# S5 preparation of a two-block network: cut into pieces behind the weight splits, with 32 powers and GpSimd's queue for its loads

## The chip, the cores and the metric

One core of one Trainium2 chip runs the whole program. The metric is the device time of one execution in microseconds. The kernel's times below are three executions; one more was taken by the hardware profiler, and every row shown comes from that one.

## The reference

Input `x` is 256 tokens by 1024. The first block has two layers, each `FFN1 -> mixer -> FFN2` with norms around them; the second block is attention, a dense FFN, attention again and a mixture of eight experts. All weights are fp32, and almost all of the time is spent on products of those weights with 256 tokens.

```python
def first_block(x, ...):
    h = x
    for i in range(DEPTH):                       # DEPTH = 2
        f = swiglu(rmsnorm(h, ffn1_pre_g[i]), ffn1_w_gate[i], ffn1_w_up[i], ffn1_w_down[i])
        h = h + 0.5 * rmsnorm(f, ffn1_post_g[i])
        m = mixer(rmsnorm(h, mix_pre_g[i]), ...)
        h = h + rmsnorm(m, mix_post_g[i])
        f = swiglu(rmsnorm(h, ffn2_pre_g[i]), ffn2_w_gate[i], ffn2_w_up[i], ffn2_w_down[i])
        h = h + 0.5 * rmsnorm(f, ffn2_post_g[i])
    return h

def s5_branch(u, lam_re, lam_im, b_re, b_im, c_re, c_im, log_step, d_skip, w_glu):
    ...
    lam_bar = jnp.exp(lam * step)                # 64 groups x 64 states, complex
    b_bar = ((lam_bar - 1.0) / lam)[..., None] * lax.complex(b_re, b_im)
    bu = jnp.einsum("blgc,gnc->blgn", ug, b_bar)
    _, states = lax.associative_scan(combine, (a_elems, bu), axis=1)   # s[t] = lam_bar * s[t-1] + bu[t]
    y = jnp.real(jnp.einsum("blgn,gcn->blgc", states, c))
```

The S5 branch of the mixer depends on the layer's input only through `u`. Everything made from `lam`, `step`, `b` and `c` alone is the "S5 preparation" of this text: it can be computed before the mixer, and both kernels do it during FFN1 (and, for one part of layer 1, during layer 0's FFN2).

## The kernel before

**The stream of weights.** A weight comes from HBM in units of 512 KB (128 x 1024 fp32). SP's queue loads a unit into a buffer `raw` (L1571 `unit`), ScalarE (ACT) copies it to `hi` (L1576), VectorE (DVE) computes `lo = raw - hi` (L1577), and TensorE (PE) makes three products per tile: `hi*hi`, `lo*hi`, `hi*lo` (L1585 to L1587, and L1591 to L1593 where weights are the stationary side). A `raw` buffer is free for the next load when its `lo` is done. `hi` and `lo` go to tiles called `big`, `part`, `hi`, `lo`; the number behind a name is the tile.

**An FFN** (`swiglu`) runs gate and up product in six chunks of columns (c0 to c5, 44 units together), then the down product (`stream_k`, 22 units d0 to d21). Chunk c0 uses `lead_b`, the others `stream_b`. Each `stream_b` unit calls `self.beside()`, which takes one step of a generator `self.side` and constrains its instructions to stand behind the unit's split (`issue_after(self.last_lo)`). The down product's last six units (`tail`) are multiplied with the first 128 tokens as they arrive and with the other 128 afterwards.

**Order.** The program is written in the order of data; a scheduler then fixes each engine's instruction order, and the queue of each engine that issues transfers, under the `issue_after` constraints. Engines run their own orders strictly in sequence. A transfer that waits for a buffer holds up what stands behind it on the same queue.

**S5 preparation in FFN1 of layer l** is a generator (`prep`) with few, large steps, placed by a table `PREP`: after chunk or unit so-and-so, take the next step. Its steps:

- `mix_prep`, layer 0 only: constants, `exp`, `sin`, `cos`, small powers (many DVE operations of 128 x 64, names `cut`, `FL`, L103 to L274), ending in the write of `lsd` to DRAM (L279, GpSimd's queue).
- `s5_wb` for each quarter q of the groups: loads `s5B` and `s5L` (L331, L333, SP's queue), four `tensor_tensor` on GpSimd (POOL, L341 to L344), and a write `Wd` (L346, GpSimd's queue). There is one buffer `s5B` and one `s5L`, so the next quarter's load waits until the `Wd` write has landed.
- `s5_cb`: loads of `s5c` (SP) and `s5b` (GpSimd) for a quarter.
- `s5_ct`: six DVE operations into `s5CF` (L372 to L377), one buffer; two ACT copies into `s5bq` (L380).
- `s5_products`: 32 pairs of small PE products into `zfa` (L396), a copy to `s5u` (L401), DVE operations that make `T` (L404 to L414), and two writes `Td` (L419, L420, GpSimd's queue).
- `s5_powers_prep(l, h)` for each half h of the groups: powers 1 to 63 of a complex number by doubling in six levels, 36 DVE operations on tiles `E` and `Et` (L301 to L303), and three writes `Ed` (L305, GpSimd's queue).

Layer 1's powers are made in layer 0's FFN2 after units d2 and d8. After FFN1 `norms` follows: its first `tensor_tensor` with `pow` on POOL (L1748), `xn` (L1771), transposes (`trfa`, L1730), and then the mixer's first product. The functions that the change touches:

Of the kernel before, what the change touches and what calls it, by code (L numbers as in the profile page):

```python
# [51 lines left out]

PREP = (
    ("c0 c1 c2 c3 c4 d0 d3 d6 d9 d12".split(), "d0 d4 d10 d15".split()),
    ("c1 c2 c4 d1 d6".split(), "c4 d1 d6 d11".split()),
)
# [22 lines left out]
class Mixer:  # L79
# [201 lines left out]
    def s5_powers_prep(self, l, h):  # L281


        g = self.nc.gpsimd
# [1 line left out]
        Ed = self.Ed[l, h] = self.dram.tile([3, P, 1024], F32, tag="Ed", name=self.nm("Ed"), bufs=4)
        if True:
            E = [self.slot("B", "E").rearrange("p (a i) -> p a i", i=64) for _ in range(3)]
            Et = self.slot("B", "Et").rearrange("p (k a i) -> p k a i", k=2, i=32)
            x, y = Et[:, 0], Et[:, 1]  # L290
# [1 line left out]
            g.memset(E[2][:, :, 0], 0.0)
            self.nc.scalar.copy(E[2][:, :, 1:], self.s4len[:, ls].unsqueeze(2).to_broadcast([P, 16, 63]))
            for r in range(2):
                g.memset(E[r][:, :, 0], 1.0 - r)
                self.nc.scalar.copy(E[r][:, :, 1], self.s4dir[:, r, ls])
            for n in (1, 2, 4, 8, 16, 32):
                k = min(n, 63 - n)
                b = [e[:, :, n : n + 1].to_broadcast([P, 16, k]) for e in E[:2]]
                for r, op in ((0, ALU.subtract), (1, ALU.add)):  # L300
                    tt(x[:, :, :k], E[0][:, :, 1 : k + 1], b[r], op=ALU.mult)  # L301
                    tt(y[:, :, :k], E[1][:, :, 1 : k + 1], b[1 - r], op=ALU.mult)
                    tt(E[r][:, :, n + 1 : n + 1 + k], x[:, :, :k], y[:, :, :k], op=op)  # L303
# [1685 lines left out]
```

## Time and profile before

| what | value |
|---|---|
| three executions | 2934.03, 2936.93, 2939.28 us; median 2936.93 |
| the profiled execution's own time | 2936.55 us |
| span of its trace | 2934.5 us |
| mean granted TensorE clock | 0.981 |
| busy, share of span: PE / DVE / ACT / POOL | 96% / 74% / 57% / 7% |

FFN1 of layer 0 runs from 11.9 (its first matmul) to 240.7, gate and up until 150.4; the mixer's first matmul is at 247.7. The other FFNs of the first block, with the same number of units: layer 0's FFN2 from 663.8 (down product from 792.6, end 852.6) and layer 1's FFN1 from 855.3 (down product from 988.3, end 1056.5, mixer's first matmul 1059.8). A row of windows gives, for a stretch, the busy time of each engine and the number of its instructions; a wait is put down to what ended it last. PEclk is the granted clock of TensorE as a share of its full 2.4 GHz. Durations of neighbouring pipelined matmuls overlap.

### The profile page before, as it was taken

How to read it: one execution, taken by the hardware profiler on the slowest of the kernel's cores; microseconds unless marked ns; L12 is line 12 of the kernel's file. 1: busy time of each engine (PE TensorE's matmuls, PEld its weight loads, DVE VectorE, ACT ScalarE, POOL GpSimd, SP SyncE). 2: the span in 40 equal slices, each digit the busy share in tenths (PEclk: the TensorE clock that was granted, in tenths of full speed). 3: DMA queues.
4: the chain of work that ended last, by engine and by line, in shares of the span. 5: the costliest groups of instructions: out<-in, count | busy, mean ns of one | idle time of the engine just before them, and what ended most of it. 6: DMA issues, size and time to landing. Idle time of an engine off the chain costs nothing. (4 is left out here: it accounts for less than half of the span.)

```text
span 2934.5 us, 49144 instructions
## 1 busy us (share of the span) xinstructions
PE 2814.3 (96%) x19040; PEld 2508.2 (85%) x19040; DVE 2181.6 (74%) x3043; ACT 1674.2 (57%) x2389; POOL 206.0 (7%) x257
## 2 busy tenths in 40 slices
PE   8979999999999999999999999999999999999997
PEld 7968888999979888888999898987678888888886
DVE  5886877765667758777755566555589999999997
ACT  5434456545445444475554445445377777777776
POOL 2140001000004100010000000000000000000000
PEclk9999999999999999999999999999899999999998
DMA  7677565576567775656855646654589999999993
GB/s 238 199 250 242 160 204 164 197 227 188 184 223 249 241 221 174 194 155 196 264 171 180 215 154 192 186 192 132 184 279 356 343 361 361 343 359 356 354 344 145
DMA packets 350928, 687.88 MB, mean 234 GB/s; under 512 B 32672, under 2 KB 121952, under 8 KB 350688
## 3 DMA queue, kind: packets, MB, share of 16 engines
q1 hardware_dynamic: 336592, 637.42, 65.9%
q0 software_dynamic: 13952, 46.74, 4.8%
q8 instruction: 151, 2.47, 0.3%
q14 instruction: 89, 0.73, 0.1%
q10 hardware_dynamic: 144, 0.52, 0.0%
HBM read 658.05 MB, written 26.54 MB: 233 GB/s over the span
## 5 line engine op out<-in xcount | busy, mean ns | idle before, releaser
L1577 DVE TENSOR_TENSOR lo<-raw,hi 128x1024 fp32r<-128x1024 f32 x646 | 788.6, 1230 | 296.8 <-ACT hi L1576 285.1
L1576 ACT CAST hi<-raw 128x1024 fp32r<-128x1024 f32 x646 | 674.9, 1048 | 455.6 <-PE accmo L1587 84.6
L1586 PE MATMUL accmo<-lo,xg 128*128 128x512 f32 (+1 forms) x768 | 289.7, 378 | 2.3 <-DVE lo L1577 2.3
L1587 PE MATMUL accmo<-hi,xg 128*128 128x512 f32 (+1 forms) x768 | 285.2, 372 | 0.0
L1585 PE MATMUL accmo<-hi,xg 128*128 128x512 f32 (+1 forms) x768 | 274.0, 373 | 1.4 <-ACT hi L1576 1.4
L1577 DVE TENSOR_TENSOR big<-raw,big 128x1024 fp32r<-128x1024 f32 x147 | 184.9, 1259 | 110.2 <-ACT big L1576 109.3
L1576 ACT CAST big<-raw 128x1024 fp32r<-128x1024 f32 x147 | 153.7, 1049 | 168.0 <-issue 31.1
L1577 DVE TENSOR_TENSOR part<-raw,part 128x1024 fp32r<-128x1024 f32 x111 | 135.3, 1223 | 85.5 <-ACT part L1576 83.1
L1576 ACT CAST part<-raw 128x1024 fp32r<-128x1024 f32 x111 | 116.1, 1050 | 114.2 <-DMA raw<-in_ffn_w_gate_dram 17.4
L1586 PEld LDWEIGHTS accmo<-lo,xg 128*128 128x128 f32 x768 | 144.6, 188 | 32.3 <-DVE lo L1577 5.6
L1585 PEld LDWEIGHTS accmo<-hi,xg 128*128 128x128 f32 x768 | 144.6, 188 | 28.1 <-ACT hi L1576 2.6
L1587 PEld LDWEIGHTS accmo<-hi,xg 128*128 128x128 f32 x768 | 144.8, 189 | 22.5
L1586 PE MATMUL accmo<-lo,th 128*128 128x512 f32 x352 | 138.0, 392 | 0.0
L1587 PE MATMUL accmo<-hi,th 128*128 128x512 f32 x352 | 137.7, 391 | 0.0
L1577 DVE TENSOR_TENSOR lo<-big,hi 128x1024 fp32r<-128x1024 f32 x88 | 106.6, 1223 | 10.7 <-ACT hi L1576 7.6
L1585 PE MATMUL accmo<-hi,th 128*128 128x512 f32 x352 | 109.2, 391 | 0.0
L1576 ACT CAST hi<-big 128x1024 fp32r<-128x1024 f32 x88 | 92.7, 1054 | 27.0 <-PE accmo L1587 26.7
L1592 PE MATMUL accfa<-xh,lo 128*128 128x256 f32 x352 | 99.8, 284 | 0.0
L1591 PE MATMUL accfa<-xh,hi 128*128 128x256 f32 x352 | 99.7, 283 | 0.0
L1593 PE MATMUL accfa<-xl,hi 128*128 128x256 f32 x352 | 99.7, 284 | 0.0
L1577 DVE TENSOR_TENSOR lo<-more,hi 128x1024 fp32r<-128x1024 f32 x68 | 82.3, 1223 | 7.0 <-ACT hi L1576 5.0
L1576 ACT CAST hi<-more 128x1024 fp32r<-128x1024 f32 x68 | 71.4, 1053 | 19.3 <-PE accmo L1587 17.8
(993 smaller groups left out, 8603.3 us busy)
## 6 DMA issues: line engine op xcount, KB each, us to landing
raw<-in_w_gu_moe_dram SPq DMA_DIRECT2D x190, 512.0 KB, 5.3
raw<-in_w_in_dram SPq DMA_DIRECT2D x128, 512.0 KB, 4.4
raw<-in_w_down_moe_dram SPq DMA_DIRECT2D x94, 512.0 KB, 5.6
raw<-in_ffn_w_gate_dram SPq DMA_DIRECT2D x88, 512.0 KB, 4.1
raw<-in_ffn_w_up_dram SPq DMA_DIRECT2D x88, 512.0 KB, 4.3
raw<-in_ffn_w_down_dram SPq DMA_DIRECT2D x88, 512.0 KB, 4.2
big<-in_w_gu_moe_dram SPq DMA_DIRECT2D x60, 512.0 KB, 5.7
more<-in_w_gu_moe_dram SPq DMA_DIRECT2D x46, 512.0 KB, 5.7
```

The lines of the kernel that those rows point to most:

```text
L1576: nc.scalar.copy(hi, raw)
L1577: self.last_lo = nc.vector.tensor_tensor(lo, raw, hi.bitcast(F32), op=ALU.subtract).ins
L1585: mm(ps, lh, rh, start=first, stop=False)
L1586: mm(ps, lh, rl, start=False, stop=False)
L1587: self.last_mm = mm(ps, ll, rh, start=False, stop=last).ins
L1591: mm(ps, lh, rh, start=first, stop=False)
L1592: mm(ps, ll, rh, start=False, stop=False)
L1593: self.last_mm = mm(ps, lh, rl, start=False, stop=last).ins
```

## The change

The steps of S5 preparation get smaller and go to `beside()`, which now also runs in the down product:

- `PREP` and `product()` are gone. Layer 0's `prep` is cut into 47 steps, layer 1's into 20. After chunk c0 (layer 0) or c1 (layer 1), every unit's split may be followed by one step; the down product's last six units have no such place. Steps that are left over after FFN1 are drained behind the last split.
- `s5_powers_prep(l)` makes powers 1 to 31 for all 32 groups at once: five levels, 30 DVE operations. Two tables of 64 columns per half are then put together on ACT: columns 32 to 63 are the powers 0 to 31, columns 1 to 31 the conjugates in reverse (`E[r][:, hs, :0:-1]`). The table is thus centred about column 32, which leaves the recurrence's result as it was. In layer 0 it comes before the quarters; layer 1's is in layer 0's FFN2 from c4 on.
- Loads of `s5B`, `s5L` and `s5c` are issued on GpSimd's queue.
- `T = K * jm` moves from DVE to ACT. The products are a step of their own.

```diff
     def s5_prep(self, I, l):
@@
         cb = [self.s5_cb(I, l, 0)]
-        yield
+        if l == 0:
+            yield from self.s5_powers_prep(0)
         for q in range(4):
             self.s5_wb(I, l, q)
             if q < 3:
                 cb.append(self.s5_cb(I, l, q + 1))
-            self.late.append(self.s5_ct(l, q, *cb.pop(0)))
-            yield
-            if l == 0 and q in (1, 2):
-                self.s5_powers_prep(0, q - 1)
-                yield
+            yield from self.s5_ct(l, q, *cb.pop(0))
@@
-        nc.sync.dma_start(B, I["s5_bT"][l, q])
+        nc.gpsimd.dma_start(B, I["s5_bT"][l, q])
         ld = self.lsd[:, p0 : p0 + 8].rearrange("k a x -> k (a x)")
-        nc.sync.dma_start(Lb, ld.unsqueeze(1).to_broadcast([8, 16, 1024]))
+        nc.gpsimd.dma_start(Lb, ld.unsqueeze(1).to_broadcast([8, 16, 1024]))
@@
-        self.nc.sync.dma_start(cc, I["s5_cT"][l, q])
+        self.nc.gpsimd.dma_start(cc, I["s5_cT"][l, q])
@@
-        nc.vector.tensor_scalar_mul(T, K, self.jm[:, 0:1])
+        nc.scalar.activation(T, K, AF.Copy, scale=self.jm[:, 0:1])
@@
             if i < nk - kk * tail:
+                self.beside()
+            if i < nk - kk * tail:
                 go(0, u, k0)
                 go(1, u, k0)
-                if aside:
-                    aside(f"d{i}")
@@
-        steps = self.prep(I, l)
-        at = PREP[l]
-
         def aside(w):
             if w == f"c{l}":
                 self.ring_drop((6, 7), (8, 9))
-            if w in at[1]:
-                self.product()
-            if w in at[0]:
-                with self.tc.issue_after(self.last_lo), self.tc.issue_after(self.last_pow.ins):
-                    next(steps, None)
-
-        return self.swiglu(*xT, *w, aside)()
+                self.side = self.prep(I, l)
+                if l == 0:
+                    with self.tc.issue_after(self.last_lo), self.tc.issue_after(self.last_pow.ins):
+                        next(self.side)
+
+        banks = self.swiglu(*xT, *w, aside)()
+        with self.tc.issue_after(self.last_lo):
+            for _ in self.side:
+                pass
+        return banks
```

The powers, new:

```python
        for n in (1, 2, 4, 8, 16):
            k = min(n, 31 - n)
            b = [e[:, :, n : n + 1].to_broadcast([P, 32, k]) for e in E]
            for r, op in ((0, ALU.subtract), (1, ALU.add)):
                tt(x[:, :, :k], E[0][:, :, 1 : k + 1], b[r], op=ALU.mult)
                ...
        for h in range(2):
            ...
            for r in range(2):
                g.memset(F[r][:, :, 0], 0.0)
                cp(F[r][:, :, 32:], E[r][:, hs])
                self.nc.scalar.activation(F[r][:, :, 1:32], E[r][:, hs, :0:-1], AF.Copy, scale=1.0 - 2.0 * r)
            g.memset(F[2][:, :, 0], 0.0)
            cp(F[2][:, :, 1:], self.s4len[:, ls].unsqueeze(2).to_broadcast([P, 16, 63]))
            for r in range(3):
                g.dma_start(Ed[r], F[r].rearrange("p a i -> p (a i)"))
```

The scheduler's order changes in three places more than the diff tells. First, DVE at the start of the program, where `xn_126` and `xn_153` are the first norm's outputs for the two halves of the tokens, and `raw_177` to `raw_223` are the first five units. Before:

```order
L1747 SCALAR_TENSOR_TENSOR sm_122<-sm_116,sm_119 128x1
L1771 SCALAR_TENSOR_TENSOR xn_126<-h_99,sm_123,gn_114 128x512 x2
L1747 SCALAR_TENSOR_TENSOR sm_149<-sm_143,sm_146 128x1
L1771 SCALAR_TENSOR_TENSOR xn_153<-h_100,sm_150,gn_114 128x512 x2
L1577 TENSOR_TENSOR big_170<-raw_177,big_170 128x1024
L1720 TENSOR_TENSOR xl_113<-tr_128,xh_112 128x4x128
L1720 TENSOR_TENSOR xl_113<-tr_136,xh_112 128x4x128
L1577 TENSOR_TENSOR big_170<-raw_187,big_170 128x1024
L1577 TENSOR_TENSOR lo_199<-raw_197,hi_198 128x1024
```

Now:

```order
L1770 SCALAR_TENSOR_TENSOR sm_122<-sm_116,sm_119 128x1
L1600 TENSOR_TENSOR big_170<-raw_177,big_170 128x1024
L1600 TENSOR_TENSOR big_170<-raw_187,big_170 128x1024
L1600 TENSOR_TENSOR lo_199<-raw_197,hi_198 128x1024
L1600 TENSOR_TENSOR lo_211<-raw_209,hi_210 128x1024
L1600 TENSOR_TENSOR lo_225<-raw_223,hi_224 128x1024
L1794 SCALAR_TENSOR_TENSOR xn_126<-h_99,sm_123,gn_114 128x512 x2
L1770 SCALAR_TENSOR_TENSOR sm_149<-sm_143,sm_146 128x1
L1794 SCALAR_TENSOR_TENSOR xn_153<-h_100,sm_150,gn_114 128x512 x2
L1743 TENSOR_TENSOR xl_113<-tr_128,xh_112 128x4x128
```

All five splits stand ahead of the norm's output now; before, only `xn` stood ahead of them.

Second, GpSimd's queue at the end of layer 0's FFN1, last quarter, from its load on (`sm_2494`, `sm_2461`: the first `pow` of the norm that follows FFN1). Before, where `s5B` and `s5L` were loaded on SP:

```order
L341 TENSOR_TENSOR s5t_2258<-s5B_2256,s5L_2257 128x1024
L420 DMA Td_2221<-s5u_2050 128x512
L483 DMA s5T_4245<-Td_1997 128x512
L342 TENSOR_TENSOR s5B_2256<-s5B_2256,s5L_2257 128x1024
L343 TENSOR_TENSOR s5B_2256<-s5B_2256,s5t_2258 128x512
L344 TENSOR_TENSOR s5B_2256<-s5B_2256,s5t_2258 128x512
L419 DMA Td_2373<-s5CF_2267 128x1024
L346 DMA Wd_2265<-s5B_2256 128x1024
L305 DMA Ed_2112<-E_2113 128x1024
L305 DMA Ed_2112<-E_2114 128x1024
L1748 TENSOR_TENSOR sm_2494<-sm_2493,mhalf 128x1
```

Now:

```order
L363 DMA Wd_1962<-s5B_1953 128x1024
L369 DMA s5b_9680<-in_s_bS_dram 128x256
L348 DMA s5B_2109<-in_s_bT_dram 128x1024
L443 DMA Td_2090<-s5u_1969 128x512
L358 TENSOR_TENSOR s5t_2111<-s5B_2109,s5L_2110 128x1024
L359 TENSOR_TENSOR s5B_2109<-s5B_2109,s5L_2110 128x1024
L368 DMA s5c_9694<-in_s_cT_dram 128x256
L442 DMA Td_2242<-s5CF_2120 128x1024
L360 TENSOR_TENSOR s5B_2109<-s5B_2109,s5t_2111 128x512
L361 TENSOR_TENSOR s5B_2109<-s5B_2109,s5t_2111 128x512
L363 DMA Wd_2118<-s5B_2109 128x1024
L1771 TENSOR_TENSOR sm_2461<-sm_2460,mhalf 128x1
```

The load of the quarter's `s5B` stands behind the previous quarter's `Wd` write on the same queue; the two `Ed` writes that stood ahead of the `pow` are gone, having moved ahead of the first quarter.

Third, DVE between the splits of the down product's last six units in layer 0 (`big_170<-raw_2343` is the first of the six, `big_170<-raw_2405` the last; L389 to L396 make `s5CF`, L433 and L437 `T`):

```order
L1600 TENSOR_TENSOR big_170<-raw_2343,big_170 128x1024
L389 TENSOR_TENSOR s5CF_2120<-s5c_1964,FL 128x8x64
L393 TENSOR_TENSOR s5CF_2120<-s5c_1964,FL 128x8x64
L433 TENSOR_TENSOR s5u_1969<-s5u_1969,dd_2083 128x8x16
L427 TENSOR_TENSOR dd_2235<-delta,sd 128x128
L1600 TENSOR_TENSOR big_170<-raw_2359,big_170 128x1024
L437 SCALAR_TENSOR_TENSOR s5u_1969<-s5u_1969,jm 128x8x48
L437 SCALAR_TENSOR_TENSOR s5u_1969<-s5u_1969,jm 128x8x32
L1600 TENSOR_TENSOR lo_2371<-raw_2369,hi_2370 128x1024
L437 SCALAR_TENSOR_TENSOR s5u_1969<-s5u_1969,jm 128x8x16
L1600 TENSOR_TENSOR lo_2383<-raw_2381,hi_2382 128x1024
L390 TENSOR_TENSOR s5u_2121<-s5c_1964,FL 128x512
```

Steps placed behind earlier units stand between these splits too.

## Rows read from the trace of the kernel before

**Rows 1.** Windows: start:end, length, busy PE, PEld, DVE, ACT, POOL, PEclk, DMA share, GB/s.

```profile
11.90:150.40 138.50, 134.31 (x994) 128.93 (x994) 107.08 (x236) 69.28 (x94) 26.34 (x36) 0.99 0.72 219
150.40:240.70 90.30, 74.67 (x521) 59.90 (x519) 78.23 (x142) 32.05 (x41) 35.07 (x35) 0.92 0.76 249
240.70:247.70 7.00, 1.80 (x9) 1.57 (x9) 5.26 (x11) 3.12 (x9) 2.41 (x3) 0.83 1.02 363
663.80:792.60 128.80, 128.56 (x985) 124.26 (x986) 74.91 (x105) 66.28 (x94) 3.59 (x11) 1.00 0.63 193
792.60:852.60 60.00, 60.00 (x267) 49.63 (x267) 47.10 (x85) 25.88 (x32) 3.75 (x7) 1.00 0.73 237
855.30:988.30 133.00, 132.53 (x1049) 127.37 (x1050) 88.67 (x99) 63.52 (x90) 41.52 (x25) 0.99 0.70 219
988.30:1056.50 68.20, 67.08 (x457) 54.95 (x455) 49.78 (x64) 30.68 (x38) 9.61 (x14) 1.00 0.82 265
1056.50:1059.80 3.30, 1.37 (x10) 0.85 (x9) 2.31 (x5) 2.03 (x7) 0.55 (x1) 1.00 0.97 318
```

**Rows 2.** Waits, 0 to 270: engine, line, waited for: total us, times, longest.

```profile
ACT hi L1576 <- DMA raw<-in_ffn_w_down_dram: 17.3, 9, 5.2
...
PE zfa L396 <- DVE s5CF L374: 7.5, 1, 7.5
...
PE trfa L1730 <- DVE xn L1771: 5.2, 1, 5.2
```

**Rows 3.** Waits of SP's queue in the same stretch.

```profile
SPq L333 <- POOL s5B L342: 19.9, 3, 9.2
SPq L331 <- DMA Wd<-s5B: 18.5, 3, 11.1
```

**Rows 4.** Timeline of the start: start us, length, engine, line, operation [idle before].

```profile
9.34 1.42 DVE L1771 SCALAR_TENSOR_TENSOR xn<-h,sm,gn 128x512 f32<-128x512 f32 x2 [1.94 <-DMA gn<-in_ffn_pre_g_dram]
...
12.82 1.22 DVE L1577 TENSOR_TENSOR big<-raw,big 128x1024 fp32r<-128x1024 f32 x1
...
14.07 5.57 SPq L1571 DMA_DIRECT2D raw<-in_ffn_w_up_dram  x4
...
19.72 1.05 ACT L1576 CAST hi<-raw 128x1024 fp32r<-128x1024 f32 x1 [0.29 <-DMA raw<-in_ffn_w_up_dram]
```

**Rows 5.** Windows, tile `E` alone (layer 0's powers): busy DVE, ACT, POOL.

```profile
140.00:240.00 100.00, 29.69 (x72) 2.94 (x6) 3.96 (x12) 0.92 0.78 260
```

**Rows 6.** The tile `Et`: min/median/max ns of its operations by line, and forms.

```profile
L301 DVE TENSOR_TENSOR Et<-E x12: 190/251/676, 156.6 to 229.0; 128x16 f32<-128x16 f32 x2, 128x32 f32<-128x32 f32 x2, 128x64 f32<-128x64 f32 x2, 128x128 f32<-128x128 f32 x2
```

**Rows 7.** Timeline, two of the power operations (256 and 496 elements).

```profile
225.50 0.42 DVE L301 TENSOR_TENSOR Et<-E 128x256 f32<-128x256 f32 x1
...
232.96 0.67 DVE L301 TENSOR_TENSOR Et<-E,E 128x496 f32<-128x496 f32 x1
```

**Rows 8.** GpSimd's timeline: first operation of quarters one and two.

```profile
126.98 2.41 POOL L341 TENSOR_TENSOR s5t<-s5B,s5L 128x1024 f32<-128x1024 f32 x1 [10.07 <-DMA s5L<-lsd]
...
146.73 3.00 POOL L341 TENSOR_TENSOR s5t<-s5B,s5L 128x1024 f32<-128x1024 f32 x1 [5.11 <-DMA s5B<-in_s_bT_dram]
```

**Rows 9.** Windows, tile `s5B` alone: POOL busy, 16 operations and 4 issues.

```profile
120.00:240.00 120.00, 38.13 (x20) 0.93 0.77 248
```

**Rows 10.** The tile `s5B`: issue to landing of the transfers from it (`Wd`).

```profile
DMA to landing us min/median/max: 5.7/7.5/10.8
```

**Rows 11.** SP's timeline: the load of the second quarter's `s5B`.

```profile
141.77 0.33 SPq L331 DMA_DIRECT2D s5B<-in_s_bT_dram  x1
```

**Rows 12.** GpSimd's timeline: an issue beside the split of rows 13, and the first `pow`.

```profile
222.88 0.58 POOL L419 DMA_DIRECT2D Td<-s5CF  x1 [3.93 <-DVE s5CF L377]
...
240.08 1.87 POOL L1748 TENSOR_TENSOR sm<-sm,mhalf 128x1 f32<-128x1 f32 x1 [0.30 <-DVE sm L1747]
```

**Rows 13.** DVE's timeline: that split, and one operation beside a GpSimd operation.

```profile
127.04 2.90 DVE L375 TENSOR_TENSOR s5CF<-s5c,FL 128x512 f32<-128x512 f32 x1
...
222.50 1.21 DVE L1577 TENSOR_TENSOR lo<-raw,hi 128x1024 fp32r<-128x1024 f32 x1
```

More of the change, by code (lines that the diff above doesn't have):

```diff
@@ L51 @@
 LEAD = 6
[L53 to L56, printed above, removed]
 EARLY = 5
@@ L234, in mix_prep @@
         cmul(*L[2], L[1], L[1])
+        yield
         cmul(*L[3], L[2], L[1])
+        yield
         cmul(*L[4], L[2], L[2])
+        yield
         den, num, lin, f = t("den"), t("num"), t("lin"), (t("fr"), t("fi"))
@@ L279, in mix_prep, with s5_powers_prep @@
         dma(self.lsd.rearrange("k a x -> a k x"), lt.rearrange("p g j r n -> p (g j) (r n)"))
-    def s5_powers_prep(self, l, h):
+    def s5_powers_prep(self, l):
         g = self.nc.gpsimd
+        cp = self.nc.scalar.copy
         tt = self.nc.vector.tensor_tensor
[L286 to L290, printed above, removed]
-            ls = slice(l * 32 + h * 16, l * 32 + h * 16 + 16)
[L292 to L303, printed above, removed]
@@ new lines, in s5_powers_prep @@
+        E = [self.slot("B", "E").rearrange("p (a i) -> p a i", i=32) for _ in range(2)]
+        Et = self.slot("B", "Et").rearrange("p (k a i) -> p k a i", k=2, i=16)
+        x, y = Et[:, 0], Et[:, 1]
+        for r in range(2):
+            g.memset(E[r][:, :, 0], 1.0 - r)
+            cp(E[r][:, :, 1], self.s4dir[:, r, l * 32 : l * 32 + 32])
+        for n in (1, 2, 4, 8, 16):
+            k = min(n, 31 - n)
+            b = [e[:, :, n : n + 1].to_broadcast([P, 32, k]) for e in E]
+            for r, op in ((0, ALU.subtract), (1, ALU.add)):
+                tt(x[:, :, :k], E[0][:, :, 1 : k + 1], b[r], op=ALU.mult)
+                if n > 8:
+                    yield
+                tt(y[:, :, :k], E[1][:, :, 1 : k + 1], b[1 - r], op=ALU.mult)
+                tt(E[r][:, :, n + 1 : n + 1 + k], x[:, :, :k], y[:, :, :k], op=op)
+                if n > 4:
+                    yield
+            if n < 8:
+                yield
@@ new lines, in s5_powers_prep @@
+        for h in range(2):
+            Ed = self.Ed[l, h] = self.dram.tile([3, P, 1024], F32, tag="Ed", name=self.nm("Ed"), bufs=4)
+            hs = slice(h * 16, h * 16 + 16)
+            F = [self.slot("B", "Eh").rearrange("p (a i) -> p a i", i=64) for _ in range(3)]
+            for r in range(2):
+                g.memset(F[r][:, :, 0], 0.0)
+                cp(F[r][:, :, 32:], E[r][:, hs])
+                self.nc.scalar.activation(F[r][:, :, 1:32], E[r][:, hs, :0:-1], AF.Copy, scale=1.0 - 2.0 * r)
+            g.memset(F[2][:, :, 0], 0.0)
+            ls = slice(l * 32 + h * 16, l * 32 + h * 16 + 16)
+            cp(F[2][:, :, 1:], self.s4len[:, ls].unsqueeze(2).to_broadcast([P, 16, 63]))
@@ L383, in s5_ct @@
             )
-        return lambda: self.s5_products(q, p0, bq, CF, s)
+        yield
+        yield
+        with self.tc.issue_after(self.last_mm):
+            self.s5_products(q, p0, bq, CF, s)
+        yield
     def s5_products(self, q, p0, bq, CF, s):
@@ L1868, in aside @@
                 self.mem_load(I)
-            if l == 0 and w in ("d2", "d8"):
-                with self.tc.issue_after(self.last_lo):
-                    self.s5_powers_prep(1, "d2 d8".split().index(w))
+            if l == 0 and w == "c4":
+                self.side = self.s5_powers_prep(1)
         return self.swiglu(*xT, *w, aside)()
@@ L1887, in prep @@
         yield from self.s5_prep(I, l)
-    def product(self):
-        with self.tc.issue_after(self.last_mm):
-            self.late.pop(0)()
     def first_body(self, I, h):
```

12 lines of the change are left out of this document (11 added, 1 removed).

## The prediction

> **What bounds the kernel now.** I first laid the first block's FFNs side by side in windows, since they stream the same number of weight units and only some carry S5 preparation [rows 1]. Layer 0's FFN2 is the yardstick: gate and up 128.8 us and down 60.0 us, PE busy in all but 0.3 of both; layer 1's step from FFN to mixer takes 3.3. Layer 0's FFN1 needs 138.5, 90.3 and 7.0: 43.7 more. Part of that is work that stays. Layer 1's down product holds three of its four product blocks and PE is busy there for 67.08, 7.08 above 60.0, so a block costs PE 2.36 and four cost 9.4. That leaves 34.3 us in layer 0's FFN1 in which PE idles or runs slowly: 9.7 in gate and up, 20.9 in down, 3.7 in the step to the mixer. Layer 1's FFN1 has 133.0, 68.2 and 3.3, 204.5 in all, against 128.8 + 60.0 + 9.4 + 3.3 = 201.5: only 3 us to be had.
>
> In the waits one sees who holds PE in layer 0: it waits 7.5 once for DVE's `s5CF` and 5.2 for `xn`, and ACT waits 17.3 for units of the down weights [rows 2]. SP's queue says why those are late: it stood 19.9 us behind the GpSimd operation that releases `s5L` and 18.5 behind the `Wd` writes that release `s5B`, with weights queued behind [rows 3]. DVE, at 78.23 of 90.3, has little slack in that stretch [rows 1].
>
> **The change, part by part** (against the profiled execution, 2936.55, which is 0.38 under the median of the three runs; what I can tell from no change is 0.2%, 5.9 us).
>
> *Start.* `xn` now stands behind five splits, the last of them of `raw_223`. That load waits for the first unit's split: before, it was issued at 14.07, when the split of 12.82 + 1.22 had ended, and its cast began at 19.72, 5.65 later [rows 4]. Now the split follows its cast directly; I put its end at 12.2 (cast 9.9 to 10.95, as the cast of 1.05 began when its unit landed, then 1.22). So 12.2 + 5.65 + 1.05 + 1.22 = 20.1 for `xn`, and as from 9.34 to 11.9 before, 2.6 more to the first matmul: about 22.5 instead of 11.9, 10.6 later. With no wait of the splits among themselves it can be 20, and with a load 2 us longer 25. Not all is lost: part of gate and up's 9.7 excess lies in the start, where the first matmuls waited for splits one by one; with five units ready PE has work from its first matmul on. These rows don't split the 9.7 (0 to 9.7 could be the start's); I take about half, 5.3, and 3 of it as remaining. Net **+8.3** (5 to 11), passed on as far as PE is the bound.
>
> *Loads on GpSimd's queue, weights unblocked.* SP's 38.4 us of standing [rows 3] go. Were PE then the bound, the mixer's first matmul would come at 22.5 + 3 + 128.8 + 60.0 + 9.4 + 3.3 = 227.0 instead of 247.7.
>
> *Powers.* 72 DVE operations, 29.69 us busy beside GpSimd [rows 5], become 30: six each at the five widths 32 to 480, 0.19, 0.22 and 0.28 (from minimum and median of the narrow ones, [rows 6]), 0.42 and 0.67 [rows 7]: 10.7 us. Widths 32 and 64 are read off between; 1 us either way. ACT gets ten copies of at most 1.05 each (a 1024-wide cast, [rows 4]) and four for `T`: up to 15 us, under its 58 idle in the down product [rows 1]. T on ACT saves DVE four operations, no more than 0.67 each [rows 7]. None of this is on the path by itself, but DVE gets some 19 us of room.
>
> *Small pieces, products in their own.* PE does the same blocks, 9.4. In the order, however, S5 operations still stand between the last six splits, so I book no gain for "none beside the last six".
>
> *What comes in its place.* GpSimd now works through one chain: first operations of a quarter, `Wd`, landing, `s5B` load, next quarter; the first `pow` of the norms stands behind the fourth. The first quarter began at 126.98 [rows 8]; it moves by the start's 8.3 and the powers' 10.7 now ahead of it: 146. A period is 38.13/4 = 9.5 for operations and `Wd`'s issue [rows 9], 7.5 for landing (5.7 to 10.8) [rows 10], 146.73 - 141.77 = 5.0 from the `s5B` load to the operation (that row's load was SP's, [rows 8, 11]), and four other issues at 0.58, 2.3 [rows 12]: 24.3. Fourth quarter: 146 + 3 x 24.3 = 218.9, + 9.5 = 228.4. The order puts a `Td` write between its operations, which waits for DVE's `s5CF`: + 2.3, as four issues. `pow` at 230.7, and as before 247.7 - 240.08 = 7.6 to the mixer [rows 12]: **238.3, that is -9.4** with the start in it. The chain is the later one against 227.0 by 11 us.
> With landing at 5.7 the chain gains 5.4, with 10.8 it loses 9.9.
> Behind the waiting `s5B` load stand `s5T`, the operations and both `Td` writes; DVE's next `s5CF` waits for `Td`, weight splits behind it. In the forecast these stalls end before the chain does.
>
> A `Td` issue took 0.58 while DVE did a split of 1.21 [rows 12, 13]; I price moved issues at that. The Trainium skill speaks against moving loads here: "SBUF — State Buffer", section "SBUF: two separate sides", says that a DMA issued from GpSimd's queue can starve for descriptors while DVE holds the shared port, and takes about 3100 ns instead of 620. By that, as an estimate, nine moved issues between the first quarter and `pow` would cost 22 us more and the total would be about 2950; the trace's row does not agree, for this kind of DVE operation.
>
> *Layer 1.* All four blocks now stand in gate and up, the down product is clean. The same GpSimd chain needs 24.3 per quarter, where the pieces come closer together. I take 204.5 + 0.5: **+0.5** (-2 to +5; the 3 us of excess can go, and the chain can hold splits for a few us).
> *Layer 0's FFN2.* Its powers cost nothing before (down product PE-bound at 60.0) and nothing now: DVE is busy 74.91 of 128.8 in gate and up [rows 1]. Without that cover they would cost 10.7. Nothing later changes.
>
> **Sum:** 2936.55 - 9.4 + 0.5 = 2927.65, **2927.7**.
>
> **Rivals.**
> *PE-bound.* Landings as quick as 5.7 and DVE's new room, so that GpSimd's chain ends in time; the mixer at 227.0: 2936.55 - 20.7 + 0.5 = 2916.4. For it: the 34.3 us of loss; against: the chain as worked out is 11 us too long.
> *The wait moves.* The chain takes the place of SP's standing. With landings at 10.8 the period is 27.6, the mixer at 248.2: 2936.55 + 0.5 + 0.5 = 2937.5, no change. For it: landing reached 10.8 once, and weights now flow beside it without gaps.
> *Slower.* Issues on GpSimd starve beside DVE. A DVE operation of usually under 0.7 was held to 2.90 beside a GpSimd one [rows 13], 2.2 more; were each of nine moved issues held as long, 19.8 us: mixer at 258, 2947.5. It decides from 1.7 us per issue, where 238.3 becomes 253.6. For it: the shared port shows in that row; against: the 0.58 of [rows 12]. This is also the price if the start costs 11 and layer 1's splits stall 5.
> *The change is not what it says.* Order shows S5 work still beside the last six units; the forecast has that in.
>
> **How the numbers follow.** Forecast 0.36, PE-bound 0.22, wait moved 0.28, slower 0.14. The forecast's own range, by landing and the start, is 2922 to 2935. The range 2915 to 2942 reaches to PE-bound on one side and past no change on the other, leaving out the slower case. Faster by over 0.2% (under 2930.7): 0.22 and most of 0.36, 0.55; same 0.29; slower (over 2942.4) 0.16.
>
> **What would show it.** Right: first matmul near 22; SP's standing behind `s5B` gone; GpSimd's quarters 24 us apart, the `pow` right behind the fourth, near 231; down product's PE waits smaller than 20.9 in sum; FFN2 unchanged at 188.8. Wrong: quarters 27 apart or issues over 1.7 us (the two worse rivals), first matmul beyond 25, or `pow` waiting for DVE and not for the queue, in which case the mixer is set by PE near 227.

## The result

The changed kernel took 2956.24 us (median of seven executions, 2948.16 to 2959.49) against 2934.03 for the kernel before on the same chip: a ratio of 1.0075, 95% interval 1.0063 to 1.0087. It is slower, where 2927.7 was forecast and a range up to 2942 given. The profiled execution took 2956.24 with a span of 2954.4, 19.9 longer than the span before. The windows of the changed kernel, in the same form as [rows 1]:

```profile
23.60:157.30 133.70, 133.70 (x1058) 128.78 (x1058) 109.25 (x264) 71.19 (x101) 24.16 (x40) 1.00 0.68 206
157.30:239.70 82.40, 71.80 (x457) 57.37 (x455) 59.22 (x55) 28.47 (x34) 36.12 (x33) 0.92 0.75 247
239.70:252.10 12.40, 1.79 (x9) 1.57 (x8) 9.23 (x17) 5.90 (x14) 2.65 (x3) 0.61 0.86 292
667.30:796.20 128.90, 128.66 (x985) 124.36 (x986) 80.89 (x115) 68.38 (x96) 4.73 (x14) 1.00 0.66 196
...
858.70:1015.90 157.20, 144.79 (x1241) 138.35 (x1242) 106.37 (x129) 69.43 (x101) 51.94 (x46) 0.93 0.67 214
1015.90:1075.80 59.90, 59.87 (x265) 49.23 (x263) 31.32 (x30) 25.93 (x29) 1.10 (x2) 1.00 0.72 220
1075.80:1080.10 4.30, 1.58 (x8) 1.23 (x8) 2.85 (x6) 2.80 (x9) 0.55 (x1) 0.85 1.00 302
```

Layer 0's FFN1 starts 11.7 later and hands over to the mixer 4.4 later (252.1 for 247.7): gate and up ends 6.9 later, the down product takes 7.9 less, the step to the mixer 5.4 more. Layer 0's FFN2 is unchanged (gate and up 128.9 for 128.8). Layer 1's FFN1 needs 157.2 + 59.9 + 4.3 = 221.4 where it needed 204.5: +16.9, the largest part of the loss. Gate and up takes 24.2 more there and the down product 8.3 less: three product blocks moved from the one to the other (7.1 at the prediction's 2.36 each), and the rest of gate and up's growth is idle time of PE (12.4, before 0.5) and a granted clock of 0.93 instead of 0.99. The rest of the program takes 1.4 less in sum. 4.4 + 16.9 - 1.4 = 19.9.

**The start** came as worked out, a microsecond later. The timeline of the changed kernel, answering to [rows 4]: SP's load, the cast, the norm's output and the first matmul:

```profile
11.40 4.72 SPq L1594 DMA_DIRECT2D raw<-in_ffn_w_up_dram  x4
...
18.75 1.04 ACT L1599 CAST hi<-raw 128x1024 fp32r<-128x1024 f32 x1 [4.28 <-DMA raw<-in_ffn_w_up_dram]
...
20.97 1.41 DVE L1794 SCALAR_TENSOR_TENSOR xn<-h,sm,gn 128x512 f32<-128x512 f32 x2
...
23.55 0.79 PE L1608 MATMUL accfa<-big,xh 128*128 128x512 f32 x1
```

The load is issued at 11.40 (12.2 was reckoned) but lands 7.3 later, not 5.65, and the first matmul is at 23.55 for 22.5.

**The powers** were priced right. All 30 DVE operations, in a window of the tile `E` alone (the first pair is the busy time and count of DVE, then ACT's):

```profile
60.00:140.00 80.00, 10.12 (x30) 4.71 (x10) 0.15 (x1) 1.00 0.70 206
```

10.12 us where 10.7 was reckoned, and 29.69 before [rows 5].

**GpSimd's chain in layer 0** began earlier than reckoned and ran slower. Its timeline, changed kernel:

```profile
141.03 2.66 POOL L358 TENSOR_TENSOR s5t<-s5B,s5L 128x1024 f32<-128x1024 f32 x1 [3.15 <-DMA Ed<-Eh]
...
153.33 0.54 POOL L363 DMA_DIRECT2D Wd<-s5B  x1
...
163.29 0.54 POOL L348 DMA_DIRECT2D s5B<-in_s_bT_dram  x1 [4.78 <-DMA Td<-s5u]
...
170.54 2.38 POOL L358 TENSOR_TENSOR s5t<-s5B,s5L 128x1024 f32<-128x1024 f32 x1 [5.20 <-DMA s5B<-in_s_bT_dram]
...
181.84 0.54 POOL L363 DMA_DIRECT2D Wd<-s5B  x1
...
194.85 0.54 POOL L348 DMA_DIRECT2D s5B<-in_s_bT_dram  x1 [11.92 <-DMA Wd<-s5B]
198.51 2.63 POOL L358 TENSOR_TENSOR s5t<-s5B,s5L 128x1024 f32<-128x1024 f32 x1 [3.13 <-DMA s5B<-in_s_bT_dram]
...
211.90 0.55 POOL L363 DMA_DIRECT2D Wd<-s5B  x1
...
223.83 0.53 POOL L348 DMA_DIRECT2D s5B<-in_s_bT_dram  x1 [9.88 <-DMA Wd<-s5B]
...
228.59 2.35 POOL L358 TENSOR_TENSOR s5t<-s5B,s5L 128x1024 f32<-128x1024 f32 x1 [3.68 <-DMA s5B<-in_s_bT_dram]
...
237.34 0.58 POOL L363 DMA_DIRECT2D Wd<-s5B  x1 [0.30 <-POOL s5B L361]
244.97 1.48 POOL L1771 TENSOR_TENSOR sm<-sm,mhalf 128x1 f32<-128x1 f32 x1 [7.05 <-DVE sm L1770]
```

The quarters start at 141.0, 170.5, 198.5 and 228.6: 29.2 apart, where 24.3 was reckoned. GpSimd's queue stood 4.8, 11.9 and 9.9 at the `s5B` loads, and each came 10.0, 13.0 and 11.9 after the issue of the `Wd` write ahead of it, where 7.5 was in the sum [rows 10]. (The first row names a `Td` write; the `Wd` write ahead landed 9.7 after its issue, at 163.0, and the load went out at 163.29.) The fourth quarter's `Wd` was issued by 237.9, 7.2 after the 230.7 reckoned for `pow`; and then `pow` waited until 244.97, for DVE. 244.97 + 7.1 = 252.1.

Why DVE came late, in ACT's, DVE's and PE's rows:

```profile
237.66 1.05 ACT L1599 CAST part<-raw 128x1024 fp32r<-128x1024 f32 x1 [4.39 <-DMA Td<-s5CF]
...
241.52 1.04 ACT L1599 CAST part<-raw 128x1024 fp32r<-128x1024 f32 x1 [1.60 <-DMA Wd<-s5B]
...
242.59 1.23 DVE L1600 TENSOR_TENSOR part<-raw,part 128x1024 fp32r<-128x1024 f32 x1 [1.49 <-ACT part L1599]
...
250.35 1.97 PE L1753 MATMUL trfa<-ident,xn 128*128 128x128 f32 x8 [10.61 <-DVE xn L1794]
```

`part` holds the mixer's first weights. Its last two casts write into buffers from which a `Td` and the fourth `Wd` write were still being read; the fourth `Wd` landed at 241.3. In DVE's order the last split stands ahead of what the norm's `pow` waits for. So the chain did set the mixer's start, but by the landing of its last write and not by the `pow` behind it on GpSimd's queue: ACT and DVE stood for it with the norm's work behind.

DVE also stood in the middle of the down product, with weight splits behind it:

```profile
193.45 0.69 DVE L389 TENSOR_TENSOR s5CF<-s5c,FL 128x512 f32<-128x512 f32 x1 [11.66 <-DMA Td<-s5CF]
...
195.93 0.79 PE L1609 MATMUL accfa<-big,hh 128*128 128x512 f32 x1 [5.38 <-DVE big L1600]
```

That `Td` write went out at 181.31 and took 12.0 to land. SP's load of the next weight unit waited 14.2 for the same split, which frees its buffer, and ACT 8.7 for that unit.

**Layer 1.** The waits of the changed kernel between 855 and 1085:

```profile
POOL s5B L348 <- DMA Wd<-s5B: 27.0, 3, 11.6
...
ACT s5u L435 <- DVE s5u L433: 20.2, 3, 9.0
...
DVE s5CF L389 <- DMA Td<-s5CF: 11.9, 2, 6.9
...
PE accfa L1614 <- DVE ht L1850: 7.8, 2, 7.2
...
PE accfa L1614 <- ACT ht L1847: 4.1, 1, 4.1
```

and one round of it in the timeline, all engines:

```profile
936.38 0.54 POOL L348 DMA_DIRECT2D s5B<-in_s_bT_dram  x1 [11.57 <-DMA Wd<-s5B]
...
943.91 0.58 POOL L442 DMA_DIRECT2D Td<-s5CF  x1
...
948.56 0.83 DVE L389 TENSOR_TENSOR s5CF<-s5c,FL 128x512 f32<-128x512 f32 x1 [6.86 <-DMA Td<-s5CF]
...
951.33 0.72 ACT L435 ACTIVATE s5u<-s5u,jm 128x512 f32<-128x512 f32 x1 [8.29 <-DVE s5u L433]
...
953.84 1.19 ACT L1847 ACTIVATE ht<-accfa 128x256 f32<-128x256 f32 x4
...
954.26 0.58 PE L1614 MATMUL accfa<-xh,hi 128*128 128x256 f32 x1 [4.07 <-ACT ht L1847]
```

It reads from the top: GpSimd's queue stands 11.57 us at the `s5B` load, for `Wd`. Behind it, once the load has landed and GpSimd's first operation on it is done, the `Td` write goes out at 943.91. DVE, which had come to the next quarter's `s5CF`, waits 6.86 for `Td`. ACT stands 8.29 in `T` behind DVE's sum, and the eviction `ht` of PE's banks stands behind `T`. PE waits 4.07.

### The profile page after: what moved, and what is told of

The parts are those of the page before. It is cut to its first block, busy times and chain, and to the rows that moved or that the text cites. A ratio compares the mean times of both kernels' runs of the same rounds, so it can differ in the third digit from the quotient of the medians.

```text
span 2954.4 us, 49061 instructions
## 1 busy us (share of the span) xinstructions
PE 2814.4 (95%) x19040; PEld 2509.6 (85%) x19040; DVE 2165.1 (73%) x2951; ACT 1687.0 (57%) x2409; POOL 215.7 (7%) x285
## 5 line engine op out<-in xcount | busy, mean ns | idle before, releaser
L1600 DVE TENSOR_TENSOR lo<-raw,hi 128x1024 fp32r<-128x1024 f32 x646 | 797.7, 1244 | 303.2 <-ACT hi L1599 292.5
L1610 PEld LDWEIGHTS accmo<-hi,xg 128*128 128x128 f32 x768 | 144.9, 189 | 22.5
L1771 POOL TENSOR_TENSOR sm<-sm,mhalf 128x1 f32<-128x1 f32 x32 | 20.7, 648 | 920.0 <-DVE sm L1770 919.9
```

The source lines that it names most:

```text
L1600: self.last_lo = nc.vector.tensor_tensor(lo, raw, hi.bitcast(F32), op=ALU.subtract).ins
L1610: self.last_mm = mm(ps, ll, rh, start=False, stop=last).ins
L1771: self.last_pow = nc.gpsimd.tensor_tensor(r, v, self.mhalf, op=ALU.pow)
```

## The experiments

Every kernel is the changed kernel or the kernel before with the edit shown or told; the order of instructions is found anew for each, so that small shifts elsewhere come with every edit. Stages from the traces, in us (layer 0: first matmul, mixer's first matmul; layer 1: FFN1's first matmul to the mixer's first), and ratios to the kernel before on the same chip with 95% intervals. A row's stages come from one execution. Where two kernels have the same order of instructions in a stage, they still differ: the mixer's start in layer 0 by up to 4.1 (241.4 for "two buffers + one split", 245.5 for "these + spread"), layer 1's FFN1 by up to 2.9 (221.4 for the changed kernel, 218.5 for "one split ahead, layer 0"). A smaller difference says nothing by itself.

| kernel | first matmul | mixer, layer 0 | FFN1, layer 1 | ratio (interval) |
|---|---|---|---|---|
| before | 11.9 | 247.7 | 204.5 | 1 |
| changed | 23.6 | 252.1 | 221.4 | 1.0075 (1.0063-1.0087) |
| Td on SP | 24.6 | 240.3 | 219.1 | 1.0044 (1.0028-1.0059) |
| layer 1 spread | 25.2 | 252.9 | 210.6 | 1.0027 (1.0017-1.0037) |
| one split ahead, every FFN | 17.3 | 240.7 | 216.4 | 1.0059 (1.0035-1.0082) |
| T on DVE | 24.7 | 247.8 | 218.3 | 1.0036 (1.0022-1.0049) |
| two s5B buffers | 24.5 | 248.4 | 214.8 | 1.0025 (1.0012-1.0037) |
| one split ahead, layer 0 | 17.1 | 247.3 | 218.5 | 1.0041 (1.0024-1.0058) |
| loads on SP | 20.2 | 244.5 | 214.4 | 1.0030 (1.0015-1.0045) |
| two buffers + one split | 17.4 | 241.4 | 215.4 | 0.9998 (0.9984-1.0013) |
| these + spread | 17.0 | 245.5 | 212.2 | 1.0016 (1.0007-1.0025) |
| these + T on DVE | 17.0 | 241.4 | 212.9 | 1.0002 (0.9990-1.0014) |
| loads on SP + spread | 20.2 | 244.0 | 206.5 | 0.9994 (0.9983-1.0004) |
| loads on SP + T on DVE | 20.2 | 238.9 | 212.2 | 1.0004 (0.9994-1.0014) |
| before + powers | 11.5 | 242.8 | 203.8 | 0.9991 (0.9982-1.0000) |
| before + loads moved | 11.3 | 248.5 | 203.0 | 1.0009 (0.9995-1.0023) |
| before + both | 11.4 | 247.5 | 201.6 | 0.9999 (0.9989-1.0009) |
| before + both + two buffers | 11.6 | 233.1 | 202.7 | 0.9944 (0.9927-0.9960) |
| the same again | 11.3 | 235.8 | 203.3 | 0.9958 (0.9943-0.9973) |
| before + loads + two buffers | 11.4 | 249.6 | 201.7 | 1.0002 (0.9992-1.0011) |

### Who is held by GpSimd's queue

Td on SP:

```diff
-        nc.gpsimd.dma_start(d[:, :1024], CF)
-        nc.gpsimd.dma_start(d[:, 1024:], T)
+        nc.sync.dma_start(d[:, :1024], CF)
+        nc.sync.dma_start(d[:, 1024:], T)
```

> Edit: the changed kernel, with the two Td writes of each quarter issued on SP's queue instead of GpSimd's. Theory 'queue': in the changed kernel a Td write stands on GpSimd's queue behind an s5B load that waits up to 11.9 us for the Wd write to land; DVE's next s5CF waits for Td (11.9 us in layer 1), ACT's T behind it (20.2 us), and the evictions of PE's banks behind both. Then layer 1's FFN1 (first matmul to the mixer's first, 221.4 us) falls to 203-209, layer 0's mixer start (252.1) to 240-249, total 2931-2942. Rival 'density': the twenty pieces of layer 1 in four chunks are too much work per weight unit whatever the queue; then layer 1 stays at 216 or more and the total at 2948 or more.

2945.74, between the two. Layer 0 did as the theory said (240.3); layer 1 did not (219.1), which was the rival's number. But its trace shows the same queue at work with another transfer. Timeline of that kernel, ACT's rows from 924 to 937 and GpSimd's from 923 to 933:

```profile
925.37 0.58 ACT L424 COPY s5u<-zfa 128x512 f32<-128x512 f32 x1
935.07 1.14 ACT L399 COPY s5bq<-s5b 128x512 f32<-128x512 f32 x2 [9.11 <-DMA s5b<-in_s_bS_dram]
936.11 0.72 ACT L435 ACTIVATE s5u<-s5u,jm 128x512 f32<-128x512 f32 x1
```

```profile
923.21 0.54 POOL L348 DMA_DIRECT2D s5B<-in_s_bT_dram  x1 [11.97 <-DMA Wd<-s5B]
...
932.62 0.60 POOL L369 DMA_DIRECT2D s5b<-in_s_bS_dram  x1
```

The `s5B` load waits 11.97; `s5b`, behind it, goes out at 932.62; ACT waits 9.11 for `s5b` in `s5bq`, with the evictions behind. The wait had changed its carrier. (In layer 0 the fourth `Wd` landed at 228.7 here, and the mixer started 11.6 later; 10.9 in the changed kernel.) So the next experiment took away what waits, not what stands behind it:

```diff
-        B, Lb = (self.slot("pp", n) for n in ("s5B", "s5L"))
+        if q % 2:
+            self.taken["pp"] += 1
+            B, Lb = self.slot("B", "s5B"), self.slot("pp", "s5L")
+        else:
+            B, Lb = (self.slot("pp", n) for n in ("s5B", "s5L"))
```

> Edit: the changed kernel, with two buffers for s5B (odd quarters take one from the shared pool), so that its load on GpSimd's queue no longer waits for the previous quarter's Wd write. Theory 'queue', refined by the run with Td on SP (there ACT waited 9.1 and 6.0 us for s5b, a load that stood behind the waiting s5B load on GpSimd's queue): it is the waiting s5B load that holds whatever stands behind it, Td in one case, s5b in the other. Then without that wait layer 1's FFN1 falls from 221.4 to 202-208, layer 0's mixer start from 252.1 to 238-245, total 2924-2934. Rival 'density': layer 1 stays above 214.

2940.59. Layer 1 fell by 6.6 to 214.8, which by the number is the rival's ("above 214") and yet well under 221.4: the held queue is a part of its loss and not all of it. One wait of 8.7 for `Wd` was left on GpSimd's queue in that stage, for 27.0 in three; PE's wait of 4.1 for ACT's `ht` was gone, and 7.4 for DVE's `ht` stayed. In layer 0 it brought 3.7 of the 7 to 14 expected, no more than the scatter.

### What the start costs

> Edit: the changed kernel, with only one split allowed ahead of the first norm's output instead of five (the constant EARLY from 5 to 1), which brings back DVE's first rows of the kernel before. 'Start counts': the first matmul goes from 23.6 to 12-13, and with all later S5 work some 7-9 us earlier the mixer's first matmul of layer 0 from 252.1 to 243-246; total 2947-2950. 'Start is hidden': the end of layer 0's FFN1 is set by a chain that the start does not move, then the mixer stays at 250-253 and the total at 2954-2958.

2952.51. "Start counts" got the direction in layer 0 and no number: the first matmul came at 17.3, not 12 to 13, the mixer at 240.7, earlier than 243 to 246, and the total is above 2950. Layer 1's FFN1 took 5.0 less (216.4), and all that follows it 11.7 more than in the changed kernel. The constant holds for those stages too; how it costs time there was not followed up. For layer 0 alone:

```diff
-                self.hold = [] if units < EARLY else self.chain[0]
+                self.hold = [] if units < self.early else self.chain[0]
@@
+            self.early = EARLY if l else 1
             banks = self.ffn1(I, l, xT)
+            self.early = EARLY
```

> Edit: the changed kernel, with one split instead of five allowed ahead of the norm's output in layer 0's FFN1 only (the run that did so for every FFN moved layer 0's mixer start to 240.7, but lost 10 us in later stages). 'Start counts': mixer start of layer 0 at 240-245, later stages as in the changed kernel, total 2943-2950. 'Start is hidden': mixer start 250-253.

2949.08, mixer at 247.3, 4.8 earlier: between "counts" and "hidden". The same start gave 240.7 in the run before it. In layer 0 the two differ in one place: with one split for every FFN, the last splits of the mixer's first weights stand behind the norm in DVE's order, and DVE no longer comes to the norm behind the fourth `Wd`. Here they stand ahead of it, and the mixer starts 10.9 after that write landed (236.4).

> Edit: both, two buffers for s5B and one split ahead of the first norm's output. If the two costs are separate places of one path they add: mixer start of layer 0 at 230-236, layer 1 at 202-208, total 2915-2925, faster than the kernel before by some 12-18 us. If the down product's end is set by something else the mixer starts at 238 or later.

2934.44: no difference from the kernel before. Layer 0 has 241.4, 10.7 less than the changed kernel (3.7 and 4.8 alone), but not 230 to 236: that is the second case, the down product's end is set by something else. Layer 1 has 215.4, not 202 to 208.

### What is left in layer 1

> Edit: the changed kernel, with T = K * jm on DVE again. 'Queue': ACT's evictions in layer 1 no longer stand behind T, so the PE wait of 4.1 that ACT ended goes or is halved, the one of 7.2 that DVE ended stays: layer 1 at 215-221, total 2950-2957. Rival 'T on ACT is the cause': layer 1 falls below 210, total under 2946.

2945.96, under the 2950 expected; layer 1 at 218.3. `T` on ACT is not the cause in layer 1. Layer 0 came out 4.3 lower, which "queue" had not said.

> Edit: the changed kernel, with layer 1's pieces taken at every second unit only, so that they reach into the down product; all on the same queues. 'Queue' and 'density' both expect layer 1's waits to go, since a quarter's pieces then take some 33 us of stream, more than the 23-27 us that GpSimd's chain needs: layer 1 at 203-208, total 2938-2944. If layer 1 stays above 215, both are wrong and something else (contention on transfers, the port shared by DVE and GpSimd) costs the time. Layer 0 is not touched: mixer at 250-254.

```diff
+        self.nth = getattr(self, "nth", 0) + 1
+        if getattr(self, "slow", False) and self.nth % 2:
+            return
         with self.tc.issue_after(self.last_lo):
             next(self.side, None)
```

2942.9; layer 1 at 210.6, above the 203 to 208 expected: 10.8 of its 16.9 went, and 6 stayed.

> Edit: the changed kernel, with the loads of s5B, s5L and s5c on SP's queue as in the kernel before. 'Queue': GpSimd's queue is no longer held, but SP's is, with weights behind it: layer 1's waits by s5b and Td go and waits of ACT for weight units take their place; layer 1 at 205-214, mixer start of layer 0 at 244-252, total 2937-2946. 'Density' alone: layer 1 at 216 or more.

2941.04. Layer 1 at 214.4, just past the upper end of "queue". With a run below (before + loads moved), layer 1's FFN1 makes a square: steps placed as before, 204.5 with the loads on SP and 203.0 on GpSimd; in pieces, 214.4 and 221.4. Moving the loads costs nothing with the old places; the pieces, with what else the change does there, cost 10, and with them the moved loads cost 7 more (4 by the 218.5 of the same order). These are the held queue, as the two buffers give 214.8 too. For the 10:

> Edit: the changed kernel with the loads on SP's queue again and layer 1's pieces at every second unit. 'Crowding': with the loads on SP the dense pieces cost layer 1 some 10 us (214.4 against 204.5 before); if that is the rate of pieces, half the rate gives 203-208. 'Placing': if it is that pieces stand between splits and the evictions of PE's banks, half the rate leaves half or more of it: 209-213. Total 2932-2940.

> Edit: the changed kernel with the loads on SP's queue again and T = K * jm on DVE. 'Coupling': if the 10 us in layer 1 come of ACT standing in T behind DVE, layer 1 falls to 204-209; if of the pieces' rate, it stays at 212-217.

Half the rate: layer 1 at 206.5 and in all 2932.22; `T` on DVE: 212.2, 2936.53. So it is the rate of the pieces. PE's waits for DVE's evictions `ht` in this stage say the same: 1.1 in the kernel before, 7.5 with the pieces and the loads on SP, 2.7 at half the rate. Where the pieces bite is seen in the timeline of the kernel with the loads on SP, DVE's, GpSimd's and PE's rows together:

```profile
920.67 0.69 DVE L395 TENSOR_TENSOR s5u<-s5c,FL 128x512 f32<-128x512 f32 x1
920.67 2.96 POOL L358 TENSOR_TENSOR s5t<-s5B,s5L 128x1024 f32<-128x1024 f32 x1 [13.01 <-PE accfa L1616]
...
921.28 2.77 DVE L437 SCALAR_TENSOR_TENSOR s5u<-s5u,jm 128x384 f32<-128x384 f32 x1
...
923.71 2.60 POOL L359 TENSOR_TENSOR s5B<-s5B,s5L 128x1024 f32<-128x1024 f32 x1
...
923.97 2.90 DVE L396 TENSOR_TENSOR s5CF<-s5CF,s5u 128x512 f32<-128x512 f32 x1
...
926.79 1.49 DVE L437 SCALAR_TENSOR_TENSOR s5u<-s5u,jm 128x256 f32<-128x256 f32 x1
...
928.20 2.28 DVE L1600 TENSOR_TENSOR big<-raw,big 128x1024 fp32r<-128x1024 f32 x1
...
932.61 0.41 DVE L1850 TENSOR_TENSOR ht<-ht,accfa 128x256 f32<-128x256 f32 x1
...
933.07 0.58 PE L1614 MATMUL accfa<-xh,big 128*128 128x256 f32 x1 [5.98 <-DVE ht L1850]
```

A DVE operation with two operands in SBUF, the on-chip memory, that starts while a GpSimd operation runs ends only after that one: L437 on 384 elements takes 2.77 and L396 2.90, where L396 took 0.69 in the changed kernel at 225.67, with GpSimd idle. Beside the quarter's four GpSimd operations, these two, the next L437 and a split took 6.4 more than such operations do alone (0.61, 0.68, 0.48 and 1.22). DVE had no gap there, so `ht` came at 932.61, and PE waited 5.98. `ht` itself, which reads one operand from PE's banks, was not held: 0.40 to 0.41 beside a GpSimd operation too. The Trainium skill, "SBUF — State Buffer", section "SBUF: two separate sides", calls the port that DVE and GpSimd share an exclusive lock, kept for the whole instruction; the rows agree. With the pieces spread and GpSimd's queue not held, a third cost showed:

> Edit: the changed kernel with three edits together: two buffers for s5B, layer 1's pieces at every second unit, one split ahead of the first norm's output. 'Queue plus density': layer 1's FFN1 was 221.4 in the changed kernel, 214.8 with two buffers, 210.6 with spread pieces; if the held queue and the crowding are two separate costs, both together give 203-207. Layer 0 as with two buffers and the start (mixer at 239-243). Total 2920-2929, faster than the kernel before by 0.2-0.5%. If layer 1 stays at 210 the two edits remove the same cost and a third one is left.

2939.84, a miss: layer 1 at 212.2, no better than spread alone (210.6). In its trace ACT waited 7.78 for one weight unit, issued about when `s5L`, `Wd`, `s5c` and `Td` went out within 2.3 us on GpSimd's queue; it took 9.6 to land, the unit before it 3.6. That the burst delayed the unit was not tried by itself.

> Edit: the same three and T = K * jm on DVE again. With the queue not held, ACT no longer waits for DVE in T: 'T couples ACT to DVE' expects another 3-8 us less in layer 0's step to the mixer and in layer 1, total 2915-2925; if ACT's T only waited because DVE was held by the queue, no difference from the run without this edit (within 4 us).

2934.85; layer 1 unchanged, layer 0 at 241.4, 4.1 less. That need not be the price of `T` on ACT: the run with two buffers and one split, which has `T` on ACT and the same order in layer 0 as the run before this one, also gave 241.4. In the two other pairs `T` on DVE gave 4.3 and 5.6 less (244.5 to 238.9), so a cost there is likely, and its size is not shown.

### The parts on their own, in the old places

```diff
-            if l == 0 and q in (1, 2):
-                self.s5_powers_prep(0, q - 1)
-                yield
+            if l == 0 and q == 1:
+                for _ in self.s5_powers_prep(0):
+                    pass
+                yield
+            if l == 0 and q == 2:
+                yield
```

(with `s5_powers_prep` of the changed kernel)

> Edit: the kernel before, with the new powers alone (30 operations for all groups once in place of 72, tables put together on ACT), in one step after the second quarter, and for layer 1 in one step after unit d2 of layer 0's FFN2. If DVE's load bounds layer 0's down product, the 19 us of DVE work saved show: mixer of layer 0 from 247.7 to 236-243, total 2922-2930. If the loads that wait on SP's queue bound it, the mixer stays at 245 or later, total 2930-2937.

2930.91: mixer at 242.8, 4.9 earlier; in all no difference that the interval shows. The 30 operations took 13.8 us here, where they stand partly beside GpSimd's.

> Edit: the kernel before, with the loads of s5B, s5L and s5c on GpSimd's queue, nothing else. 'Queue': there the steps of layer 1 stand far apart, and a held GpSimd queue delays Td and s5b, not weights: layer 1 at 203-210, and layer 0's mixer at 240-250, as ACT's 17.3 us of waits for weights go and waits for Td come; total 2928-2942. If moved loads alone explain the loss of the changed kernel, total above 2948.

2933.55: layer 0 unchanged, layer 1 at 203.0. Moved loads alone explain nothing of the loss. Together:

> Edit: the kernel before with the new powers and the loads of s5B, s5L and s5c on GpSimd's queue, the steps and their places as before. Powers alone gave layer 0's mixer at 242.8, loads alone 248.5 and 203.0 for layer 1. If the gain of the powers is held back by SP's standing queue: mixer at 234-240, total 2920-2927; if the two do not add, mixer at 241-246, total 2927-2933.

2934.98, mixer at 247.5, later than both cases had it: they don't add. GpSimd's queue stood 18.5 us at `s5B` loads in layer 0 of that trace. And with two buffers beside both:

> Edit: as the run before it, with two buffers for s5B. If the waiting s5B load is what is left in layer 0, mixer another 3-8 us earlier than in the run before it, total 2915-2925; if bursts of transfers or DVE's products are, within 3 us of it.

**2919.13**, ratio 0.9944 (0.9927 to 0.9960), faster than both kernels; the mixer came 14.4 earlier than in the run before it, where 3 to 8 were expected. Its windows, layer 0's gate and up, down, and step to the mixer (compare [rows 1]):

```profile
11.60:148.00 136.40, 132.72 (x993) 127.71 (x993) 103.37 (x235) 67.73 (x93) 28.70 (x40) 0.99 0.72 215
148.00:225.80 77.80, 73.16 (x522) 59.24 (x520) 68.36 (x95) 38.08 (x50) 38.49 (x45) 0.96 0.84 285
225.80:233.10 7.30, 1.83 (x10) 1.61 (x9) 7.19 (x16) 2.75 (x9) 1.37 (x2) 0.68 0.99 352
```

The down product takes 77.8 for 90.3, PE idle there for 4.6 instead of 15.6.

> The same program as the fastest run so far (kernel before, new powers, loads on GpSimd's queue, two buffers for s5B), once more with more rounds on this chip: 2916-2923, ratio to the kernel before 0.993-0.997 if it holds; 0.998 or more if the first measurement was an outlier.

2922.87, ratio 0.9958 (0.9943 to 0.9973): it holds, a little smaller.

> Edit: the same without the new powers: kernel before, loads on GpSimd's queue, two buffers for s5B, 72 power operations as before. 'The held queue alone held layer 0': mixer of layer 0 at 233-238, total 2920-2926, the powers then bring little. 'Both are needed': mixer at 240-246, total 2927-2934, as powers alone brought 5 us and loads alone nothing.

2933.81, mixer at 249.6: without the powers the unheld queue brings nothing. Both are needed. That each alone leaves the other's wait as the last one is argued; the new powers and two buffers with the loads left on SP were not tried.

## Why the prediction was wrong

- **Start: right.** First matmul 23.6 for 22.5; gate and up took 133.7, and less the 128.8 of the yardstick and one product block of 2.4 that leaves 2.5, where 3 was taken.
- **Powers: right in price** (10.12 for 10.7; they now stand where GpSimd is idle). "None of this is on the path by itself" held in the main: alone, 16 us less of DVE's work moved the mixer by 4.9, hardly more than the scatter, and the total not beyond its interval.
- **The first quarter: early.** 141.0 where 146 stood in the sum.
- **The period: mis-sized.** "7.5 for landing" measured 9.7, 12.7 and 11.7; 24.3 became 29.2. Three periods make 14.7 more, the early start takes 5 back; with the fourth quarter's operations and issues 2.5 quicker than reckoned, the chain ended 7.2 late.
- **The chain's end: the wrong path.** The sum let the mixer follow `pow`, and `pow` the issue of the fourth `Wd`. But `pow` waited 7.05 more, for DVE, which stood behind the landing of the last `Td` and of that write: their buffers go to the mixer's first weights, and this wait was not in the sum. 7.2 + 7.05 - 0.5 for a quicker last step make the 13.8 by which layer 0 came out above the forecast. It is 3.9 above the rival "the wait moves" (248.2), which had the long landings and not the end. The sign "`pow` waiting for DVE and not for the queue" came true, and the mixer was not near 227 for it: it was still the chain that DVE waited for.
- **"Weights unblocked": the step that did not happen.** SP no longer stood behind `s5B` and `s5L`, but ACT waited 25.4 for units of the down weights in layer 0's FFN1 where it had waited 17.3 [rows 2]. The prediction named the wait that did it, DVE's next `s5CF` for `Td` with weight splits behind it, and priced it at nothing ("in the forecast these stalls end before the chain does"): DVE stood 11.66 there, PE 5.38.
- **Layer 1, "+0.5 (-2 to +5)": the step that failed.** It was +16.9. The prediction named what stands behind the waiting `s5B` load, and that "the pieces come closer together" than the chain's 24 us, and still took it for a few us. The square of runs shows some 10 from the rate of the pieces and 4 to 7 from the held queue.
- **"Slower": right sign, wrong mechanism.** Its rival rested on issues that starve beside DVE. The issues of the moved loads took 0.53 to 0.67 in the changed kernel, near the 0.58 of [rows 12]; the 3100 ns that the Trainium skill states in "SBUF — State Buffer", section "SBUF: two separate sides", for a DMA beside a DVE `tensor_copy`, did not show in them. The prediction was wrong to read that section as speaking against the move here: of `tensor_tensor`, which both DVE operations of [rows 13] are, it says that its probe did not show the stall. What cost time was not the issue of a transfer but the wait ahead of it.

## What to carry to other kernels

A load moved to an idle engine's queue takes its wait along: count what stands behind it on the new queue and who waits for that, and give the load a buffer of its own before moving it. If one of several transfers behind the wait is moved away, the next one carries it. Cutting work into pieces behind each split does not lower its rate: here half the rate took back 8 of 10 us in layer 1. And a chain does not end with the issue of its last write: ask who takes over the buffer, and what stands behind that one.

## Not expected

Each of the two good parts, fewer powers (mixer of layer 0 at 242.8) and an unheld queue (249.6), brought little or nothing, and both together 12 to 15 us (235.8, 233.1). In the changed kernel's layer 0 a `Wd` write of 512 KB took 9.7 to 12.7 us to land when a 512 KB load of `s5L` stood right ahead of it, and 5.7 to 10.8 in the kernel before, where that load was on SP [rows 10]. The load ahead is not the whole cause: with `Td` on SP it stood there too, and the same writes took 7.0 to 7.8. What went out together landed together: the six transfers that were issued from 180.1 to 182.4 in the changed kernel, a weight unit of SP's among them, landed from 190.8 to 194.9. That unit took 9.5; the ones issued at 179.05 and 202.25 took 3.6 and 3.4. That the crowd is the cause, and which of the six held the others, was not tried.
